# Forgetting attention: logit biases loaded from shifted copies in place of being added up on GpSimd

## The chip, the cores and the metric

The kernel runs on one core of one Trainium2 chip. A core has TensorE (PE, matrix products into PSUM), VectorE (DVE), ScalarE (ACT), GpSimd (POOL) and SyncE (SP), each with an instruction queue of its own that is worked through in order; semaphores tie the queues together. SyncE issues almost all transfers between HBM and the on-chip memory SBUF; 16 DMA engines carry them. The metric is device time in microseconds for one execution, the median over several runs; lower is better.

## The reference

A decoder trunk of two layers over 512 tokens of width 1024, in float32. Layer 0 mixes tokens with a gated unit (gMLP), layer 1 with Forgetting Attention (FoX, 16 heads of 64); each is followed by a squared-ReLU MLP of width 4096, and every part adds to the residual `x`. The change lies in the attention alone:

```python
q, k, v, gate, f_logit = jnp.split(h @ w_in, [W, 2 * W, 3 * W, 4 * W], axis=-1)
...
log_f = jax.nn.log_sigmoid((f_logit + b_f).astype(jnp.float32))
c = jnp.cumsum(log_f, axis=1).transpose(0, 2, 1)
...
for i in range(S // Q_BLOCK):
    q0 = i * Q_BLOCK
    kend = q0 + Q_BLOCK
...
    logits = jnp.einsum('bhtd,bhsd->bhts', qb, kb).astype(jnp.float32) * scale
    logits = logits + c[:, :, q0:kend, None] - c[:, :, None, :kend]
    logits = jnp.where(t_idx >= s_idx, logits, -jnp.inf)
    probs = jax.nn.softmax(logits, axis=-1).astype(vb.dtype)
```

`c` holds, for each head, the running sum over tokens of the log forget gates. A logit of query t and key s gets `c[t] - c[s]`. The term `c[t]` is the same over a whole row, and a softmax doesn't change when a constant is added to a row.

## The kernel before

Every weight is split into a high and a low part (`wh`, `wl`), and each product is made of three matmuls (`mm3`). Weights come in chunks through `Stream`: SyncE loads a chunk into one of three `raw` buffers (line 80), ScalarE rounds it into `wh` (line 85), and the rest `wl` is formed (line 86), in the attention stage by GpSimd, in the others by VectorE. The next load into a `raw` buffer waits for the `wl` that read it last. `wh` and `wl` have four buffers each, and the stream runs three chunks ahead of use.

The attention stage (`fs` and `fp` pools, lines 605 to 902) works on 8 pairs of heads, p = 0 to 7, and 4 blocks of 128 queries, i = 0 to 3. Block i sees keys 0 to (i+1)·128. `project` makes queries, keys and values of a pair; its tail takes the mean squares of queries and keys (`yss`), raises them to a power on GpSimd (line 725) and scales `y` on VectorE (line 726). `forget`, run once with pair 0, makes the log forget gates, sums them by two matmuls into `pc`, keeps the negative sums in `ct` (queries on partitions; line 645), transposes them into `pct`, copies them to `cs` (heads on partitions, line 651) and writes `cs` to HBM as `cd` (line 652).

`attend` then works on one pair. It transposes `y` (`tq`, `tk`), forms `qs`, `ks`, `kl`, and for each of its two heads, e = 0 and 1, with hd = 2p + e: loads `cd[hd]` broadcast over all 128 partitions into `cb` (line 785), and for each block GpSimd adds `ct` to a stretch of `cb` (line 792) and masks the diagonal (line 794) to get `bias`. TensorE makes the logits `lg` with the sign turned round, VectorE adds the bias and takes the row minimum (line 803, `ee` and `mn`), ScalarE takes the exponential with its row sum (line 804), and VectorE scales by the reciprocal of that sum (lines 806 and 808). The `bias` tiles have one buffer for each i, `cb` has two. The weights `ee` are transposed (`tp`, line 840), split into `pth` and `ptl` (lines 842, 843) and multiplied with the values (`ot`); the result is gated (line 828) and split (lines 859, 860).

Several of these generators run interleaved with the projections. `advance` steps the one that is due by the counter `order["us"]`, which only `placed` moves, that is only matmuls and transposes of this stage; those are kept in the order of the program. The other engines' orders are fixed when the program is built, by a planner that has its own estimate of when things are ready and prefers what comes first in the program. Tiles of one tag share that tag's buffers: a tile that takes a buffer waits until the last reader of the tile before is done.

Of the kernel before, what the change touches and what calls it, by code (L numbers as in the profile page):

```python
# [8 lines left out]
F32 = mybir.dt.float32  # L9
F32R = mybir.dt.float32r  # L10
AF = mybir.ActivationFunctionType
ALU = mybir.AluOpType
# [4 lines left out]
P = 128  # L17
D = 1024
S = 512
KB = D // P  # L20
NT = S // P
E = 2 * D
FF = 4 * D
H = 16
# [114 lines left out]
def trunk(ctx: ExitStack, tc: tile.TileContext, A, out, stages=4):  # L139
    nc = tc.nc  # L140
    pe, dve, act, pool = nc.tensor, nc.vector, nc.scalar, nc.gpsimd
# [6 lines left out]
    dram = ctx.enter_context(tc.tile_pool(name="dram", bufs=1, space=DRAM))  # L148
# [4 lines left out]
    def psB(name):  # L153
        return ps.tile([P, S], F32, tag="B", name=name, bufs=3)

    def psD(name):
        return ps.tile([P, S], F32, tag="D", name=name, bufs=1)
# [83 lines left out]
    def mm(dst, a, b, start, stop, more=False):  # L241

        ins = pe.matmul(dst, a, b, start=start, stop=stop, skip_group_check=more)  # L243
        placed(ins, dst.shape[-1])
        return ins

    def turn(dst, src):
        placed(pe.transpose(dst, src, ident[: src.shape[0], : src.shape[0]]), 256)  # L248
# [357 lines left out]
    with ExitStack() as st:  # L606
        fs = st.enter_context(tc.tile_pool(name="fs", bufs=2))
        fp = st.enter_context(tc.tile_pool(name="fp", bufs=2))
# [11 lines left out]
        for e in range(2):  # L620
            dve.memset(kl[e][(1 - e) * DH : (2 - e) * DH].bitcast(F32), 0.0)
        ct = fp.tile([P, NT, H], F32, tag="ct", name="ct", bufs=1)
        cd = dram.tile([H, S], F32, tag="cd", name="cd")

        def forget(pq):

            fl = fp.tile([P, NT, H], F32, tag="fl", name="fl", bufs=1)
            for i in range(NT):
                dve.scalar_tensor_tensor(fl[:, i], pq[i][:, 3 * P : 3 * P + H], nm.rstd[:, i : i + 1], bf, op0=ALU.mult, op1=ALU.add)
            ff = fl.rearrange("p i h -> p (i h)")  # L630
            fa = fp.tile([P, NT * H], F32, tag="fa", name="fa", bufs=1)
            dve.scalar_tensor_tensor(fa, ff, -1.0, ff, op0=ALU.mult, op1=ALU.min)
            act.activation(fa, fa, AF.Exp)
            act.activation(fa, fa, AF.Ln, bias=1.0)
            dve.scalar_tensor_tensor(ff, ff, 0.0, fa, op0=ALU.min, op1=ALU.subtract)

            pre = fp.tile([P, NT, H], F32, tag="pre", name="pre", bufs=1)
            dve.memset(pre[:, 0], 0.0)
            for i in range(1, NT):
                dve.tensor_tensor(pre[:, i], pre[:, i - 1], fl[:, i - 1], op=ALU.add)  # L640
            yield LAG_FORGET, None
            pc = psD("pc")
            mm(pc[:, : NT * H], tri, ff, True, False)
            mm(pc[:, : NT * H], ones, pre.rearrange("p i h -> p (i h)"), False, True)
            dve.tensor_scalar(ct.rearrange("p i h -> p (i h)"), pc[:, : NT * H], -1.0, None, op0=ALU.mult)
            yield LAG_PT, None
            pt = psD("pct")
            for i in range(NT):
                turn(pt[:H, i * P : (i + 1) * P], ct[:, i])
            cs = fp.tile([H, S], F32, tag="oz", name="cs")  # L650
            act.activation(cs, pt[:H], AF.Copy, scale=-1.0)
            nc.sync.dma_start(cd, cs)
            did.add("F")

        epsr = small.tile([P, NT], F32, tag="epsr", name="epsr")
# [35 lines left out]
        def project(p, values=True):  # L691
# [9 lines left out]
            if p == 0:  # L701
                dve.tensor_scalar(epsr, nm.ms, RMS_EPS, None, op0=ALU.mult)
                running.append([order["us"], forget(pq), None])
                advance(True)
                gates[0] = gate_act(0, gates[0])
                did.add(("G", 0))
# [18 lines left out]
            pool.tensor_tensor(sf, sf, mhalf, op=ALU.pow)  # L725
            dve.tensor_tensor(yh, yh, sf.unsqueeze(2).to_broadcast([P, NT * 4, DH]), op=ALU.mult)  # L726
            running.append([order["us"] + LAG_NORM, attend(p, y), None])

        def gate_act(p, pg):
# [28 lines left out]
        def attend(p, y):  # L758
# [21 lines left out]
            for e in range(2):  # L780
                hd = 2 * p + e
                yield lag, ("T", p - 1, e) if p else "F"
                lag = 0.0
                cb = fp.tile([P, S], F32, tag="cb", name=f"cb{hd}")
                nc.sync.dma_start(cb, cd[hd].partition_broadcast(P))
                ees = []
                sm = fs.tile([P, NT], F32, tag="sm", name=f"sm{hd}")
                mn = fs.tile([P, NT], F32, tag="mn", name=f"mn{hd}")
                for i in range(NT):
                    n = (i + 1) * P  # L790
                    bi = fp.tile([P, n], F32, tag=f"bias{i}", name=f"bias{hd}_{i}", bufs=1)
                    pool.tensor_scalar(bi, cb[:, :n], 1.0, ct[:, i, hd : hd + 1], op0=ALU.mult, op1=ALU.add)
                    dg = bi[:, i * P :]
                    pool.affine_select(dg, dg, pattern=[[-1, P]], compare_op=ALU.is_ge, fill=BIG, base=0, channel_multiplier=1)
                    yield lag, None
                    lag = LAG_LOGIT * rush
                    ee = fp.tile([P, n], F32, tag=f"ee{i}", name=f"ee{hd}_{i}", bufs=2)
                    ees.append(ee)
                    lg = psB(f"lg{hd}_{i}")
                    ts_ = slice(i * P, (i + 1) * P)  # L800
                    mm(lg[:, :n], qs[e][:, ts_], ks[e][:, :n], True, False)
                    mm(lg[:, :n], qs[e][:, ts_], kl[e][:, :n], False, True)
                    dve.tensor_tensor_reduce(ee, lg[:, :n], bi, 1.0, 3.0e38, op0=ALU.add, op1=ALU.min, accum_out=mn[:, i : i + 1])
                    act.activation(ee, ee, AF.Exp, bias=mn[:, i : i + 1], scale=-1.0, accum_out=sm[:, i : i + 1])
                rc = fs.tile([P, NT], F32, tag="rc", name=f"rc{hd}")
                dve.reciprocal(rc, sm)
                for i in range(NT):
                    dve.tensor_scalar(ees[i], ees[i], rc[:, i : i + 1], None, op0=ALU.mult)  # L808
                soft.append(ees)
                did.add(("L", p, e))  # L810
# [19 lines left out]
            for e in range(2):  # L830
                hd = 2 * p + e
# [4 lines left out]
                for j in range(NT):  # L836
                    n = (NT - j) * P
# [118 lines left out]
def build(arrays, stages=4):  # L956
    import concourse.bacc as _bacc

    nc = _bacc.Bacc("TRN2", target_bir_lowering=False, num_devices=1)
    args = {}  # L960
    for name, a in arrays.items():
        args[name] = nc.dram_tensor(f"in_{name}_dram", a.shape, mybir.dt.from_np(a.dtype), kind="ExternalInput").ap()
    out = nc.dram_tensor("out_0_dram", (D, S), F32, kind="ExternalOutput").ap()
    with tile.TileContext(nc, schedule_with_timeline_sim=True) as tc:
        trunk(tc, args, out, stages)
    return nc
# [9 lines left out]
```

## Time and profile before

| | us |
|---|---|
| median of 3 runs | 1277.18 |
| lowest, highest | 1276.97, 1279.51 |
| the profiled execution, time | 1277.01 |
| the profiled execution, span of its instructions | 1275.3 |

The page gives the span, the busy time of each engine, and groups of instructions by line of the kernel. "Idle before" is the time in which an engine had nothing to run before an instruction of the group, and the name behind the arrow is what ended that. The timeline view lists instructions as start, duration, engine, line, operation, output and inputs, shape and count, with the idle time before in brackets. The windows view gives, for a stretch, the busy time of PE, PEld (weight loads of TensorE), DVE, ACT and POOL, then the granted clock, the share of time in which the DMA engines were busy, and GB/s. In the views of waits the numbers behind the colon are microseconds in total, how many times, and the longest. Lines of DMA issues have the size of each and the median time from issue to landing. SPq is SyncE's queue.

### The profile page before, as it was taken

How to read it: one execution, taken by the hardware profiler on the slowest of the kernel's cores; microseconds unless marked ns; L12 is line 12 of the kernel's file. 1: busy time of each engine (PE TensorE's matmuls, PEld its weight loads, DVE VectorE, ACT ScalarE, POOL GpSimd, SP SyncE). 2: the span in 40 equal slices, each digit the busy share in tenths (PEclk: the TensorE clock that was granted, in tenths of full speed). 3: DMA queues.
4: the chain of work that ended last, by engine and by line, in shares of the span. 5: the costliest groups of instructions: out<-in, count | busy, mean ns of one | idle time of the engine just before them, and what ended most of it. 6: DMA issues, size and time to landing. Idle time of an engine off the chain costs nothing.

```text
span 1275.3 us, 18354 instructions
## 1 busy us (share of the span) xinstructions
PE 1262.1 (99%) x7108; PEld 1114.0 (87%) x7108; DVE 877.2 (69%) x1206; ACT 624.9 (49%) x981; POOL 484.7 (38%) x415
## 2 busy tenths in 40 slices
PE   9999999999999999999999999999999999999998
PEld 7888888888999999998899899898888999999987
DVE  7347767677867676765537777777887767676763
ACT  7334423246534344443467687678465444444430
POOL 4108433025423232310657667667173322323200
PEclk9999999999999999999999999999999999999999
DMA  7333233233233332323223222223223323232321
GB/s 250 97 107 92 83 91 91 84 98 93 90 116 100 100 102 97 111 89 96 80 81 103 84 82 76 84 77 106 83 67 116 116 84 116 84 116 83 118 81 66
DMA packets 39607, 124.01 MB, mean 97 GB/s; under 512 B 4816, under 2 KB 5840, under 8 KB 39520
## 3 DMA queue, kind: packets, MB, share of 16 engines
q1 hardware_dynamic: 39232, 122.82, 30.4%
q8 instruction: 56, 0.92, 0.3%
q14 instruction: 31, 0.25, 0.1%
q10 hardware_dynamic: 288, 0.02, 0.0%
HBM read 120.69 MB, written 2.13 MB: 96 GB/s over the span
## 4 chain that ended last, share of the span: by engine, by line
PE 89%; DVE 6%; ACT 2%; issue 1%; POOL 1%; DMA 1%; DVEq 0%; ACTq 0%; POOLq 0%
PE po L243 36%; PE da L243 11%; PE bc L243 9%; PE pq L243 8%; PE pv L243 8%; PE pu L243 7%; PE ph L243 3%; PE pg L243 2%; PE ot L243 2%; DVE xl L271 1%; PE lg L243 1%; PE tp L248 1%; PE sp L426 1%; DVE ee L808 1%; DVE y L726 1%
## 5 line engine op out<-in xcount | busy, mean ns | idle before, releaser
L85 ACT ACTIVATE wh<-raw 128x1024 fp32r<-128x1024 f32 (+3 forms) x230 | 219.7, 957 | 270.9 <-PE po L243 83.5
L86 DVE TENSOR_TENSOR wl<-raw,wh 128x1024 fp32r<-128x1024 f32 (+1 forms) x178 | 252.5, 1432 | 46.2 <-ACT wh L85 45.4
L243 PE MATMUL po<-zl,wh 128*128 128x512 f32 x512 | 200.6, 392 | 1.3 <-DVE zl L500 1.3
L243 PE MATMUL po<-zh,wh 128*128 128x512 f32 x512 | 199.9, 391 | 0.0
L243 PE MATMUL po<-zh,wl 128*128 128x512 f32 x512 | 199.5, 390 | 0.0
L556 DVE TENSOR_TENSOR x<-x,po 128x512 f32<-128x512 f32 x128 | 87.2, 683 | 106.1 <-PE po L243 106.1
L86 POOL TENSOR_TENSOR wl<-raw,wh 128x768 fp32r<-128x768 f32 (+3 forms) x52 | 102.4, 1969 | 125.7 <-ACT wh L85 123.2
L110 POOL TENSOR_TENSOR ssum<-raw 128x512 f32<-128x512 f32 x26 | 35.5, 1364 | 268.6 <-DMA raw<-in_m_dram 256.8
L85 ACT ACTIVATE sh<-ssum 128x1024 fp32r<-128x1024 f32 x52 | 55.2, 1061 | 164.5 <-POOL ssum L111 95.8
L243 PEld LDWEIGHTS po<-zh,wl 128*128 128x128 f32 x512 | 96.2, 188 | 19.5
L243 PEld LDWEIGHTS po<-zh,wh 128*128 128x128 f32 x512 | 96.5, 188 | 17.9
L243 PEld LDWEIGHTS po<-zl,wh 128*128 128x128 f32 x512 | 96.6, 189 | 17.8 <-DVE zl L500 1.6
L243 PE MATMUL pq<-wh,xh 128*128 128x384 f32 (+2 forms) x256 | 88.4, 345 | 0.0
L410 POOL TENSOR_SCALAR vn<-v,mv,lnr 128x128 f32<-128x128 f32 x64 | 63.1, 999 | 59.5 <-DVE vl L414 59.4
L243 PE MATMUL pq<-wh,xl 128*128 128x384 f32 (+2 forms) x256 | 83.1, 325 | 0.0
L243 PE MATMUL pq<-wl,xh 128*128 128x384 f32 (+2 forms) x256 | 82.7, 323 | 0.0
L86 DVE TENSOR_TENSOR sl<-ssum,sh 128x1024 fp32r<-128x1024 f32 x52 | 65.9, 1268 | 18.2 <-ACT sh L85 18.1
L112 POOL TENSOR_TENSOR ssum<-raw,ssum 128x512 f32<-128x512 f32 x26 | 37.1, 1428 | 69.1 <-DVE sl L86 68.8
L243 PE MATMUL da<-th,sl 128*128 128x256 f32 x208 | 58.9, 283 | 0.0
L243 PE MATMUL da<-tl,sh 128*128 128x256 f32 x208 | 58.8, 283 | 0.0
L243 PE MATMUL pv<-wh,xh 128*128 128x512 f32 (+1 forms) x160 | 58.0, 372 | 0.7 <-ACT wh L85 0.7
L243 PE MATMUL pv<-wl,xh 128*128 128x512 f32 (+1 forms) x160 | 58.7, 368 | 0.0
(212 smaller groups left out, 3489.9 us busy)
## 6 DMA issues: line engine op xcount, KB each, us to landing
raw<-in_m_dram SPq DMA_DIRECT2D x128, 512.0 KB, 3.6
raw<-in_gw_u_dram SPq DMA_DIRECT2D x16, 512.0 KB, 3.5
raw<-in_gw_o_dram SPq DMA_DIRECT2D x16, 512.0 KB, 3.5
raw<-in_fw_qkv_dram SPq DMA_DIRECT2D x20, 384.0 KB, 3.0
raw<-in_gw_v_dram SPq DMA_DIRECT2D x14, 512.0 KB, 3.9
raw<-in_fw_g_dram SPq DMA_DIRECT2D x8, 512.0 KB, 3.4
cb<-cd SPq DMA_DIRECT2D x16, 256.0 KB, 3.3
raw<-in_fw_o_dram SPq DMA_DIRECT2D x8, 512.0 KB, 3.5
```

The source lines that it names most:

```text
L85: self.nc.scalar.activation(hi, t, AF.Copy)
L86: eng.tensor_tensor(lo, t, hi.bitcast(F32), op=ALU.subtract)
L110: tt(s12[:, 0], a21, a22, op=ALU.add)
L112: tt(s43[:, 0], a12, s12[:, 1], op=ALU.subtract)
L243: ins = pe.matmul(dst, a, b, start=start, stop=stop, skip_group_check=more)
L248: placed(pe.transpose(dst, src, ident[: src.shape[0], : src.shape[0]]), 256)
L271: dve.scalar_tensor_tensor(l, x[b], gcol, h.bitcast(F32), op0=ALU.mult, op1=ALU.subtract)
L410: pool.tensor_scalar(vn[:, i], v[i][:, cb * P : (cb + 1) * P], mv[:, i, 0:1], lnr[:, i : i + 1], op0=ALU.subtract, op1=ALU.mult)
L426: pe.matmul(dst, vh[:, 2 * c + i], wide, start=True, stop=False)
L556: dve.tensor_tensor(x[b], x[b], pt, op=ALU.add)
L726: dve.tensor_tensor(yh, yh, sf.unsqueeze(2).to_broadcast([P, NT * 4, DH]), op=ALU.mult)
L808: dve.tensor_scalar(ees[i], ees[i], rc[:, i : i + 1], None, op0=ALU.mult)
```

## The change

`forget` no longer writes one copy of the running sums. VectorE makes four, one for each block of queries: the sums up to the end of the block, less the sum at the block's first token. Each is written to its own place in `cd`. For each head and block, one transfer then brings that copy's row, broadcast over the partitions, straight into the `bias` tile; GpSimd's addition of `ct` goes, and its masking of the diagonal stays. What differs from the bias before is a constant for each row, which the softmax takes out again. `cb` goes; `bias` tiles of the first three blocks have two buffers, that of the fourth has one. The shifted copies pass through the same buffers.

```diff
-        cd = dram.tile([H, S], F32, tag="cd", name="cd")
+        cd = dram.tile([H, NT, S], F32, tag="cd", name="cd")
+
+        def bias_tile(i, name):
+            return fp.tile([P, (i + 1) * P], F32, tag=f"bias{i}", name=name, bufs=2 if i < 3 else 1)
...
             act.activation(cs, pt[:H], AF.Copy, scale=-1.0)
-            nc.sync.dma_start(cd, cs)
+            for i in range(NT):
+                n = (i + 1) * P
+                shifted = bias_tile(i, f"cs{i}")
+                dve.tensor_scalar(shifted[:H], cs[:, :n], cs[:, i * P : i * P + 1], None, op0=ALU.subtract)
+                nc.sync.dma_start(cd[:, i, :n], shifted[:H])
             did.add("F")
...
-                cb = fp.tile([P, S], F32, tag="cb", name=f"cb{hd}")
-                nc.sync.dma_start(cb, cd[hd].partition_broadcast(P))
+                bias = []
+                for i in range(NT):
+                    bias.append(bias_tile(i, f"bias{hd}_{i}"))
+                    nc.sync.dma_start(bias[i], cd[hd, i, : (i + 1) * P].partition_broadcast(P))
...
                 for i in range(NT):
                     n = (i + 1) * P
-                    bi = fp.tile([P, n], F32, tag=f"bias{i}", name=f"bias{hd}_{i}", bufs=1)
-                    pool.tensor_scalar(bi, cb[:, :n], 1.0, ct[:, i, hd : hd + 1], op0=ALU.mult, op1=ALU.add)
+                    bi = bias[i]
                     dg = bi[:, i * P :]
```

## The prediction

> **What bounds the kernel now.** I read the busy times first, then what TensorE waits for in the attention stage, then what stands in front of those waits.
>
> ```profile
> span 1275.3 us, 18354 instructions
> PE 1262.1 (99%) x7108; PEld 1114.0 (87%) x7108; DVE 877.2 (69%) x1206; ACT 624.9 (49%) x981; POOL 484.7 (38%) x415
> ...
> 655.00:900.00 245.00, 239.36 (x1471) 219.63 (x1471) 180.92 (x417) 183.73 (x392) 162.94 (x178) 1.00 0.28 87
> ...
> PE tp L248 <- DVE ptl L843: 3.6, 4, 1.9
> PE tq L248 <- DVE y L726: 1.0, 2, 0.7
> PE ot L243 <- DVE v L677: 0.6, 1, 0.6
> ```
>
> The third line is the row of the windows view for 655 to 900 us, the stretch in which the biases are made: TensorE (PE) is busy 239.4 of 245 us, VectorE (DVE) 180.9, GpSimd (POOL, the last number with a count) 162.9, at full clock. The last three lines are, but for 0.2 us, all that TensorE waits for between 640 and 900 us: 5.2 us, every time for VectorE, never for GpSimd, a DMA or a weight. So TensorE bounds this stage too, and the change touches none of its work. The order of matmuls is set by a counter that only matmuls and transposes advance, and the change leaves every `yield` where it was, so I take TensorE's order as unchanged. What the change can give is part of those 5.2 us. What it can take is larger.
>
> **What is removed.**
>
> ```profile
> L792 POOL TENSOR_SCALAR bias<-cb,ct 128x128 f32<-128x128 f32 (+1 forms) x64 | 38.4, 606 | 18.1 <-DVE mn L803 12.3 <-DVE kl L775 4.6 <-DVE yss L724 1.2
> L794 POOL TENSOR_SCALAR_AFFINE_SELECT bias<-bias 128x128 f32<-128x128 f32 x64 | 22.0, 355 | 1.3
> ...
>   POOL bias L794: 1.5, 2
> ...
> POOL wl L86 <- ACT wh L85: 69.0, 22, 5.6
> ACT wh L85 <- PE po L243: 9.0, 4, 4.4
> ACT wh L85 <- PE pq L243: 8.7, 5, 4.2
> ```
>
> The 64 additions go: 38.4 us of GpSimd, whose load in the stretch falls from 162.9 to about 124.5. The 64 masks stay. Directly this is worth almost nothing: VectorE stood idle for a bias for 1.5 us, twice (third line, from the view of the tile `bias`). Nor is the weight path short of GpSimd: it waits 69 us for ScalarE's halves (`wh`), and ScalarE waits for TensorE to free their buffers (last two lines). Weights are ahead of use, so earlier `wl` gives nothing.
>
> The gain is indirect: VectorE runs slower while GpSimd is busy.
>
> ```profile
> 707.13 2.74 DVE L808 TENSOR_SCALAR ee<-ee,rc 128x128 f32<-128x128 f32 x4
> ...
> 712.16 1.27 DVE L808 TENSOR_SCALAR ee<-ee,rc 128x128 f32<-128x128 f32 x4
> ...
> 706.33 1.85 POOL L86 TENSOR_TENSOR wl<-raw,wh 128x768 fp32r<-128x768 f32 x1
> 708.15 1.07 POOL L792 TENSOR_SCALAR bias<-cb,ct 128x256 f32<-128x256 f32 x2
> 709.19 0.83 POOL L794 TENSOR_SCALAR_AFFINE_SELECT bias<-bias 128x128 f32<-128x128 f32 x2
> 711.83 2.91 POOL L725 TENSOR_TENSOR yss<-yss,mhalf 128x16 f32<-128x16 f32 x1
> ...
> 714.78 0.30 PE L248 MATMUL tp<-ident,ee 128*128 128x128 f32 x1 [1.87 <-DVE ptl L843]
> ```
>
> The same four scalings of one head took 2.74 us beside GpSimd's `wl`, additions and masks, and 1.27 us beside its power (L725). The excess is 1.47 us. Shared out by overlap (1.05 us of `wl`, 1.07 of additions, 0.68 of masks), the additions' part is 1.07/2.80 x 1.47 = 0.56 us. It lies in VectorE's queue ahead of the largest wait of TensorE, 1.87 us at 714.78, so I take it as **0.56 us saved**. The second place is the last pair:
>
> ```profile
> 884.49 2.04 DVE L808 TENSOR_SCALAR ee<-ee,rc 128x128 f32<-128x128 f32 x4
> ...
> 884.89 0.59 POOL L794 TENSOR_SCALAR_AFFINE_SELECT bias<-bias 128x128 f32<-128x128 f32 x2
> 885.47 0.78 POOL L792 TENSOR_SCALAR bias<-cb,ct 128x512 f32<-128x512 f32 x1
> 886.22 2.54 POOL L86 TENSOR_TENSOR wl<-raw,wh 128x1024 fp32r<-128x1024 f32 x1
> ...
> 887.19 0.50 PE L243 MATMUL ot<-pth,v 128*128 128x512 f32 x1 [0.62 <-DVE v L677]
> ```
>
> Here the excess is 2.04 - 1.27 = 0.77 us, and the addition covers 0.75 of the 2.04 us, so 0.75/2.04 x 0.77 = **0.28 us saved** ahead of a wait of 0.62. Elsewhere VectorE's saving ends in no wait of TensorE, or the slow neighbour is `wl`, which stays. The bounds of this term: nothing, if `wl` moves into the freed place and slows VectorE there instead; and the whole of the waits that lie behind attention work, 3.6 + 0.6 + 0.3 = 4.5 us (of the two waits for `y` the longer, 0.7, is the first pair's, and its `y` starts when L725 ends). I take 0.8 because that is what overlap shows.
>
> The page GPSIMD Engine Reference of the Trainium skill (section Specifications) limits this contention to VectorE instructions that use both ports or two SBUF inputs. By it the scalings and `y` gain but the additions of logits and bias (L803), with one input in PSUM, do not; if the rule were void and L803 gained too, the sum would only move towards the fast rival.
>
> **What is added at the start.** Four VectorE subtractions on 16 partitions, 128 to 512 columns, and four writes in place of one.
>
> ```profile
> 659.59 0.57 ACT L651 ACTIVATE cs<-pct 16x512 f32<-16x512 f32 x1
> ...
> 660.00 2.85 DVE L726 TENSOR_TENSOR y<-y,yss 128x1024 f32<-128x1024 f32 x1 [1.72 <-POOL yss L725]
> 664.32 0.74 DVE L774 SCALAR_TENSOR_TENSOR qs<-tq,qkn,qs 64x512 fp32r<-64x512 f32 x1 [1.47 <-ACT qs L771]
> ...
> cd<-cs SPq DMA_DIRECT2D x1, 32.0 KB, 2.0
> cb<-cd SPq DMA_DIRECT2D x16, 256.0 KB, 3.3
> ```
>
> The nearest row is again the scaling of four blocks: 1.27 us as the value, 2.74 as the upper end, nothing as the lower. `cs` is finished at 660.16, when VectorE has begun `y` at 660.00; behind `y` it idles 1.47 us up to 664.32. I put the subtractions there, 662.85 to 664.12: **0 us**. If the order of VectorE were made the other way round, `y` would start at 660.16 + 1.27 = 661.43, and TensorE, which waits for `y`, would lose 1.4 us.
>
> The writes then land by about 664.1 + 2.0 = 666.1, and the first block's bias (64 KB, between the rows for 32 and 256 KB, so 2.0 to 3.3) by 668.1 to 669.4; with the mask of 0.36 us it is ready by 669.8 at the latest. The last block's bias, three SyncE (SP) issues of about 0.4 us later, is ready by 671.0.
>
> ```profile
> 669.23 0.29 DVE L803 CUSTOM_DVE_ANT_0 ee<-lg,bias 128x128 f32<-128x128 f32 x1
> ...
> 671.23 0.56 DVE L803 CUSTOM_DVE_ANT_0 ee<-lg,bias 128x384 f32<-128x384 f32 x1 [0.96 <-POOL bias L794]
> 672.74 0.69 DVE L803 CUSTOM_DVE_ANT_0 ee<-lg,bias 128x512 f32<-128x512 f32 x1 [0.94 <-PE lg L243]
> ```
>
> So the first head may start 0.6 us late, and VectorE's own idle 0.96 and 0.94 us in the third and fourth block take that up: 0 us. Without that cover it would be 0.6.
>
> **What is added per head.** Each head now loads 64 + 128 + 192 + 256 = 640 KB in place of 256: 16 x 384 KB = 6.3 MB more, 26 GB/s beside 87, so DMA engines busy 0.28 go to about 0.36. The 48 more issues hold SyncE 16 us in all (0.33 each); behind them in its queue stand weight loads, which have the cover shown above. These are **0 us**.
>
> The new wait that matters is that of the fourth block. Its bias has a single buffer, so for the second head of a pair the load is issued only when VectorE has used the first head's. Queued behind it on SyncE are weight loads; queued behind its mask on GpSimd are `wl` and the power. Who waits for it is VectorE's queue. The price: landing 3.3 us (the first line below, of the view of the tile `cb`, has 3.0 to 4.3) plus mask 0.36, so 3.66 us, or 4.66 at the worst landing. The distances are those between two 512-column rows of L803:
>
> ```profile
> DMA to landing us min/median/max: 3.0/3.3/4.3
> ...
> 679.62 0.68 DVE L803 CUSTOM_DVE_ANT_0 ee<-lg,bias 128x512 f32<-128x512 f32 x1
> ...
> 704.04 0.68 DVE L803 CUSTOM_DVE_ANT_0 ee<-lg,bias 128x512 f32<-128x512 f32 x1
> ...
> 710.38 0.68 DVE L803 CUSTOM_DVE_ANT_0 ee<-lg,bias 128x512 f32<-128x512 f32 x1
> ...
> 857.34 0.69 DVE L803 CUSTOM_DVE_ANT_0 ee<-lg,bias 128x512 f32<-128x512 f32 x1
> ...
> 862.30 0.68 DVE L803 CUSTOM_DVE_ANT_0 ee<-lg,bias 128x512 f32<-128x512 f32 x1
> ```
>
> In pair 0 there are 679.62 - 673.43 = 6.2 us (the first head's stands above, at 672.74), in pair 1 710.38 - 704.72 = 5.7, in pair 6, the shortest that I found, 862.30 - 858.03 = 4.3. The slack is 2.5, 2.0 and 0.6 us (1.0 less at the worst landing, so at most 0.4 lost in pair 6): **0 us**, as long as SyncE is free when the buffer is. [...] The three smaller biases have two buffers and are free a pair earlier.
>
> **Sum.** 0.56 + 0.28 = 0.84 saved, nothing lost. The profiled execution took 1277.01 us (1.7 beside its span), the median of the three is 1277.18; 1277.0 - 0.8 = **1276.2 us**. A measurement can tell about 0.2% (2.55 us) from no change, so this counts as none.
>
> **The rivals.**
> *Slower: the fourth block's load is stuck behind a weight load.* SyncE takes its queue in order, and a weight load at its head waits for `wl`.
>
> ```profile
> 708.20 0.33 SPq L80 DMA_DIRECT2D raw<-in_fw_qkv_dram  x1
> ...
> 863.09 3.48 SPq L80 DMA_DIRECT2D raw<-in_fw_o_dram  x2
> ```
>
> If pair 1's load stands behind the one at 708.20, it is issued at 708.53 and ready at 712.2: 1.8 us after 710.38. Pair 6's behind 863.09 is issued at 863.42 and ready at 867.1: 4.8 us late. Together 6.6 us, counted in full since VectorE is behind TensorE there: 1276.2 + 6.6 = 1282.8. It decides from an issue 2.0 us (pair 1) or 0.6 us (pair 6) after the buffer comes free. For it: the slack is thin, the order is fixed when the program is built. Against: `wl` comes earlier on a lighter GpSimd, so these loads do too.
> *Faster: nearly all waits behind VectorE go*, since `wl` also moves out of the scalings' way: 4.5 us less, 1272.5. For it: scalings took 1.27 to 2.74 us. Against: `wl` is the larger part of the overlap and stays.
> *Unchanged to slightly slower*: `wl` slides into the freed place, or the subtractions go ahead of `y`: 1277.0 to 1278.4.
>
> **Chances.** Forecast 0.42, unchanged 0.08, faster rival 0.22, slower rival 0.28. The forecast and the unchanged case lie within 0.2%. So faster 0.22, same 0.50, slower 0.28. The range takes in both rivals with a microsecond for their sizes: 1271.5 to 1284.0; the likeliest case's own is 1274.8 to 1278.4.
>
> **What would show it.** Right: GpSimd down by about 38 us, L808 shorter in the mean, TensorE's wait at `tp` in pair 1 shorter than 1.87 us, no bias named among VectorE's waits, `y` starting at 660. Wrong: VectorE waiting for a mask at a 512-column L803, or a bias load issued right behind a weight load and microseconds after its buffer was free (slow rival); TensorE's waits for VectorE near 1 us (fast rival); TensorE's instructions in another order, which would void the whole sum.

## The result and the profile after

The changed kernel took **1285.59 us** (median of 5 runs, 1284.54 to 1289.51) against 1277.18 before (5 runs, 1276.26 to 1279.51): a ratio of 1.0068, with a 95% interval of 1.0049 to 1.0087. It is slower by 8.4 us, where 1276.2 was forecast. The profiled execution took 1284.54 us with a span of 1282.8, so its trace holds 7.5 us of the 8.4. Its granted clock is 1.000; the other four runs have 0.997 to 0.999.

First the page of the kernel after: the span, and the busy time of each engine.

```profile
span 1282.8 us, 18419 instructions
...
PE 1263.2 (98%) x7108; PEld 1114.7 (87%) x7108; DVE 879.3 (69%) x1210; ACT 624.6 (49%) x981; POOL 448.2 (35%) x351
```

GpSimd does 36.5 us less (484.7 before), as forecast. No engine does noticeably more, and the number of TensorE's matmuls and their order are the same. So the 7.5 us are waits. The windows view of the stretch from 655 to 900 us, and the view of what TensorE waited for between 600 and 960 us (total, times, longest):

```profile
655.00:900.00 245.00, 231.37 (x1430) 213.24 (x1429) 175.18 (x407) 180.39 (x386) 121.09 (x113) 1.00 0.36 111
```

```profile
PE tp L248 <- DVE ptl L852: 8.6, 7, 2.0
PE ot L243 <- DVE v L685: 2.7, 1, 2.7
PE tq L248 <- DVE y L734: 1.1, 2, 0.7
PE tq L248 <- DVE ptl L852: 0.6, 1, 0.6
...
PE ot L243 <- DVE oz L836: 0.5, 1, 0.5
PE po L243 <- DVE v L685: 0.4, 1, 0.4
```

TensorE is busy 231.4 us of the 245 where it was 239.4. The waits are 13.9 us where they were 5.2: 8.7 more, all for VectorE. (The span grows by 7.5 only; a wait for `zl` later in the kernel falls from 1.3 to 0.2 us.) Set side by side matmul by matmul, the two traces show where TensorE falls behind: by 1.9 us in pair 0, by 1.0 to 1.2 in each of pairs 1, 2 and 3, by 2.9 in the last pair, and by little elsewhere. VectorE is hardly busier (879.3 us, 877.2 before), so it must be late: it waits itself. For whom, the view of all waits from 640 to 930 us of the kernel after says:

```profile
POOL bias L803 <- DMA bias<-cd: 39.0, 24, 6.5
...
DVE y L734 <- POOL yss L733: 9.4, 6, 2.6
...
DVE ee L812 <- POOL bias L803: 4.6, 4, 1.8
```

and the same view of the kernel before:

```profile
DVE y L726 <- POOL yss L725: 3.7, 4, 1.7
...
DVE ee L803 <- POOL bias L794: 1.5, 2, 1.0
```

GpSimd, which has less to do, stands still for 39 us with a mask (line 803) at the head of its queue, waiting for its bias to land. VectorE in turn waits 9.4 us for GpSimd's power and 4.6 us for masks, 5.2 before. Here is one such place, the end of pair 0, in the timeline of the kernel after (start, duration, in brackets the idle time before and what ended it; first SyncE, then GpSimd, then VectorE):

```profile
675.44 0.33 SPq L80 DMA_DIRECT2D raw<-in_fw_g_dram  x1
675.87 0.38 SPq L795 DMA_DIRECT2D bias<-cd  x1
```

```profile
678.71 0.29 POOL L803 TENSOR_SCALAR_AFFINE_SELECT bias<-bias 128x128 f32<-128x128 f32 x1 [2.03 <-DMA bias<-cd]
678.97 1.84 POOL L86 TENSOR_TENSOR wl<-raw,wh 128x768 fp32r<-128x768 f32 x1
...
685.89 0.29 POOL L803 TENSOR_SCALAR_AFFINE_SELECT bias<-bias 128x128 f32<-128x128 f32 x1 [0.47 <-DMA bias<-cd]
686.15 1.83 POOL L86 TENSOR_TENSOR wl<-raw,wh 128x768 fp32r<-128x768 f32 x1
687.95 2.90 POOL L733 TENSOR_TENSOR yss<-yss,mhalf 128x16 f32<-128x16 f32 x1
```

```profile
681.09 0.69 DVE L812 CUSTOM_DVE_ANT_0 ee<-lg,bias 128x512 f32<-128x512 f32 x1 [1.82 <-POOL bias L803]
...
690.88 3.40 DVE L734 TENSOR_TENSOR y<-y,yss 128x1024 f32<-128x1024 f32 x1 [2.56 <-POOL yss L733]
```

In the order of GpSimd's queue the mask at 678.71 belongs to pair 1, whose logit for it comes 26 us later (704.88); its load was issued early because its buffer was free. GpSimd waits 2.03 us for it. Behind it stand `wl`, and behind that the mask of pair 0's fourth block, which VectorE needs now: VectorE idles 1.82 us. The queue is only part of this wait. The fourth block's own load was issued at 675.87, 2.1 us after its single buffer came free (673.76), right behind a weight load on SyncE (675.44), and took 4.6 us to land, until 680.5: with nothing ahead of it on GpSimd its mask would have been some 0.3 us earlier. Then more masks of pair 1, the last one at 685.89 waiting for its landing, and another `wl` stand ahead of pair 1's power, whose input was ready at 685.7 (line 732 ends there) and which starts at 687.95. `y` is late by as much, and VectorE's queue has `y` ahead of the `ptl` that TensorE needs next. TensorE loses 1.55 us at 685.66 (0.42 before) and 0.62 at 694.80 (none before).

In pair 1 a mask of pair 2 holds `wl` back by 2.83 us:

```profile
709.56 0.43 POOL L803 TENSOR_SCALAR_AFFINE_SELECT bias<-bias 128x128 f32<-128x128 f32 x1 [2.83 <-DMA bias<-cd]
```

That `wl` falls upon pair 1's scalings: 2.90 us for four that take 1.27 beside the power (714.50 in this same trace: 1.28). That is little more than the 2.74 us of before, and TensorE's wait behind them, 1.97 us at 717.12, was 1.87. What the change adds in pair 1 comes next, by the same second mechanism on another instruction:

```profile
717.24 1.84 POOL L86 TENSOR_TENSOR wl<-raw,wh 128x768 fp32r<-128x768 f32 x1
```

```profile
717.35 2.81 DVE L734 TENSOR_TENSOR y<-y,yss 128x1024 f32<-128x1024 f32 x1
```

```profile
720.55 0.55 PE L248 MATMUL tp<-ident,ee 128*128 128x128 f32 x3 [1.66 <-DVE ptl L852]
```

A mask that waited 0.50 us for its landing stands ahead of `wl`, which so starts just before `y`. `y` takes 2.81 us beside it (1.22 in e1 below, without a `wl` beside it), and now stands ahead of a `ptl` that came before it in the kernel before; TensorE waits 1.66 us for that `ptl`, where it waited 0.71 for the next one.

The last pair shows the second mechanism alone: no mask waits, but GpSimd, free of additions, starts `wl` at once.

```profile
891.18 2.56 POOL L86 TENSOR_TENSOR wl<-raw,wh 128x1024 fp32r<-128x1024 f32 x1 [0.33 <-ACT wh L85]
```

```profile
890.39 3.63 DVE L817 TENSOR_SCALAR ee<-ee,rc 128x128 f32<-128x128 f32 x4
```

```profile
895.16 0.50 PE L243 MATMUL ot<-pth,v 128*128 128x512 f32 x1 [2.69 <-DVE v L685]
```

Before, masks and the 512-column addition (884.89 to 886.22) stood ahead of that `wl`, and the four scalings took 2.04 us; TensorE waited 0.62 at the same place.

### The profile page after: what moved, and what is told of

Same layout as the page of the kernel before. It is cut to its first block, busy times and chain, and to the rows that moved or that the text cites. A ratio compares the mean times of both kernels' runs of the same rounds, so it can differ in the third digit from the quotient of the medians.

```text
span 1282.8 us, 18419 instructions
## 1 busy us (share of the span) xinstructions
PE 1263.2 (98%) x7108; PEld 1114.7 (87%) x7108; DVE 879.3 (69%) x1210; ACT 624.6 (49%) x981; POOL 448.2 (35%) x351
## 4 chain that ended last, share of the span: by engine, by line
PE 85%; DVE 7%; POOL 2%; DMA 2%; ACT 2%; issue 1%; SPq 0%; POOLq 0%; DVEq 0%; ACTq 0%
PE po L243 36%; PE da L243 11%; PE bc L243 9%; PE pv L243 7%; PE pu L243 7%; PE pq L243 7%; PE ph L243 3%; DMA bias<-cd 2%; PE ot L243 1%; PE pg L243 1%; DVE xl L271 1%; DVE y L734 1%; POOL yss L733 1%; DVE ee L817 1%; PE lg L243 1%
```

## The experiments

Four explanations were put against each other. **A**: masks wait for landings in GpSimd's queue, and hold up what stands behind them. **B**: the single buffer of the fourth block makes its load late. **C**: the added transfers, or SyncE's 48 more issues, cost the time. **D**: `wl` falls on VectorE's scalings and stops them. In the diffs, "after" is the changed kernel. Each was timed against the kernel before in the same session (1277.05 to 1277.25 there).

**e1: the masks of a pair behind that pair's power** (A). TensorE's and ScalarE's orders stay as they are; on VectorE two neighbours change places, on SyncE one weight load.

```diff
-            pool.tensor_tensor(sf, sf, mhalf, op=ALU.pow)
+            powers[p] = pool.tensor_tensor(sf, sf, mhalf, op=ALU.pow).ins
...
-                    pool.affine_select(dg, dg, ...)
+                    with tc.issue_after(powers[p]):
+                        pool.affine_select(dg, dg, ...)
```

> The changed kernel, but on GpSimd the masks of a pair stand behind that pair's power (L733), so that a mask for the next pair, whose bias is still in flight, can no longer stand in front of the power or of weight rests that are wanted now. Theory A (GpSimd's queue is held up by masks that wait for a landing): about 1277, at most 1279, GpSimd's idle time for landings of bias falls from 39 us to under 15, and the power of the second pair starts within 0.3 us of its input instead of 2.3 us after. Theory B (the single buffer of the fourth block is what is late): nothing changes, 1284 to 1287, since the fourth block's wait in a pair stays. Theory C (the additional transfers and SyncE's longer queue): 1284 to 1287.

Measured: 1278.08 us (11 runs, 1277.02 to 1281.66), ratio 1.0011 (1.0002 to 1.0020): 7.5 of the 8.4 us are gone, with the same masks, the same transfers and the same buffers. TensorE's waits, and GpSimd's masks from 655 to 908 us (busy, mean ns, then the idle time before them and its causes), in this kernel:

```profile
PE tp L248 <- DVE ptl L853: 3.7, 5, 1.8
PE ot L243 <- DVE v L685: 2.7, 1, 2.7
```

```profile
L804 POOL TENSOR_SCALAR_AFFINE_SELECT bias<-bias 128x128 f32<-128x128 f32 x64 | 24.3, 410 | 24.7 <-DMA bias<-cd 24.6
```

The waits at `tp` are back at 3.7 us (8.6 after, 3.6 before), though the trace is that of the longest of the eleven runs (1281.66). GpSimd still waits 24.6 us for landings (under 15 was expected), but the power no longer stands behind them: VectorE waits 3.4 us for it, 9.4 before the edit. In pair 0 a wait of 1.82 us at `tp` stays: the fourth block's mask itself waits 3.40 us for its landing there (682.49). The wait at `ot` is untouched: 2.7.

**e2, e4: no masks at all**, in the kernel after (e2) and, as a control, in the kernel before (e4).

```diff
-                    pool.affine_select(dg, dg, ...)
```

> The changed kernel without the 64 masks of the diagonal (left out, so the weights above the diagonal are not zero). GpSimd then waits for no landing at all; VectorE waits for the loads itself. Theory A: 1274 to 1278. Theory B: the fourth block's load is still issued late; 1282 to 1286. Theory C: 1283 to 1286. To be read against the kernel before without its masks.

> The kernel before without its 64 masks (left out, as in the run above). It is the yardstick for that run: 22 us of GpSimd go in both. All theories: 1274 to 1277.5. Theory A has the two within 2 us of each other; theory C has the changed kernel without masks some 8 us longer; theory B 5 to 8.

Measured: the kernel after without masks 1279.65 us (11 runs), ratio 1.0019 (1.0010 to 1.0028), 1.7 us above the range of A; its wait at `ot` is still 2.7. The kernel before without masks **1287.54** (5 runs), ratio 1.0078 (1.0065 to 1.0090): 22 us of GpSimd's work left out, no wait for a landing anywhere, and 10 us slower. That was a surprise, and it speaks for D. The control's waits of TensorE, and its last pair:

```profile
PE tp L248 <- DVE ptl L842: 8.8, 7, 2.5
PE ot L243 <- DVE v L677: 3.2, 1, 3.2
```

```profile
889.74 2.40 POOL L86 TENSOR_TENSOR wl<-raw,wh 128x1024 fp32r<-128x1024 f32 x1
```

```profile
888.64 3.71 DVE L807 TENSOR_SCALAR ee<-ee,rc 128x128 f32<-128x128 f32 x3
```

Three scalings begun at 888.64 end at 892.35, just after `wl` (892.14). The two kernels also speak against C: without masks the kernel after, with all its transfers and issues, is 8 us faster than the kernel before. e13 below settles it: it has them all and is faster than the kernel before with its masks.

**e3: two buffers for the fourth block** (B); the second block gives one up for room.

```diff
-            return fp.tile([P, (i + 1) * P], F32, tag=f"bias{i}", name=name, bufs=2 if i < 3 else 1)
+            return fp.tile([P, (i + 1) * P], F32, tag=f"bias{i}", name=name, bufs=1 if i == 1 else 2)
```

> The changed kernel with two buffers for the biases of blocks 1, 3 and 4 and one for the second block (the memory does not hold two for all). Theory A: 1283 to 1287, even more masks can stand ahead. Theory B: the loss of the fourth block goes; 1280 or less, no wait of VectorE for a mask at a 512-column row. Theory C: 1284 to 1287.

Measured: 1287.44 us (5 runs, 1283.77 to 1289.27), ratio 1.0074 (1.0061 to 1.0088): not faster. GpSimd waits even longer for landings, 45.1 us. B falls as the explanation of the 8.4 us. In pair 0 it does hold: the logits of the fourth block no longer wait for a mask there (679.53), and TensorE's wait at `tp` is 0.78 us in place of 1.55. Next to it, at `tq`, 0.62 became 2.24. The trace's waits add up to 14.1 us, 13.9 in the kernel after; with them goes a granted clock of 0.91 in the stretches 680 to 700 and 740 to 760 us, where the trace of the kernel after has 1.00. The run moves the single buffer to another block rather than taking it away, so it says nothing on a kernel with two buffers everywhere.

**e8: the addition kept as idle work**: does more GpSimd work keep `wl` off the scalings, as the additions did before?

```diff
+                    pool.tensor_scalar(bi, bi, 1.0, None, op0=ALU.mult)
                     pool.affine_select(dg, dg, ...)
```

> The changed kernel with GpSimd's 38 us put back: each bias, loaded finished, is multiplied by 1 in place before its mask (64 instructions of the same shapes). Theory D in its plain form (GpSimd's removed work had kept the rests away from VectorE's scalings): back towards 1277 to 1281. Theory A: the additional instructions wait for the same landings and hold the queue longer, 1286 to 1292. Theory C: 1285 to 1288.

Measured: 1305.3 us (5 runs), ratio 1.0223 (1.0209 to 1.0237). That lies above every range given for it (A had 1286 to 1292). More work on GpSimd as such protects nothing: here it waits for landings too (26.5 us), in the same queue, and makes everything behind it later still. This fits A; why it costs so much more than A foresaw stays open.

**m1: the standstill by itself** (D): a small kernel in place of the decoder, twelve VectorE instructions of each kind, first alone (`q_`), then while GpSimd works through 24 subtractions of 1024 columns (`b_`).

> No decoder at all: it leaves out the whole computation and hands x through. Four kinds of VectorE instruction, twelve of each, first with GpSimd idle and then beside a row of GpSimd subtractions of 128x1024. Theory D: the scaling with one SBUF input (128x512) takes about 0.48 us alone and 2 to 3 us beside GpSimd; the sum of two SBUF inputs 0.6 to 0.7 alone and more beside; the sum with one input in PSUM the same both times. If the slowing were a plain sharing of bandwidth, all with SBUF inputs would slow by one factor under 2 instead.

Measured, in its groups by line (busy us, mean ns of one):

```profile
L52 POOL TENSOR_TENSOR w<-w,w 128x1024 f32<-128x1024 f32 x24 | 60.9, 2536 | 1.9
L42 DVE TENSOR_TENSOR b_two_in<-x,x 128x512 f32<-128x512 f32 x12 | 32.6, 2720 | 0.4
L40 DVE TENSOR_SCALAR b_one_in<-x,one 128x512 f32<-128x512 f32 x12 | 27.4, 2281 | 0.4
L42 DVE TENSOR_TENSOR q_two_in<-x,x 128x512 f32<-128x512 f32 x12 | 8.3, 691 | 0.4
L44 DVE TENSOR_TENSOR q_psum<-bank,x 128x512 f32<-128x512 f32 x12 | 8.3, 690 | 0.4
L44 DVE TENSOR_TENSOR b_psum<-bank,x 128x512 f32<-128x512 f32 x12 | 8.3, 690 | 0.4
L40 DVE TENSOR_SCALAR q_one_in<-x,one 128x512 f32<-128x512 f32 x12 | 5.8, 486 | 0.4
```

A scaling of 512 columns takes 486 ns alone and 2281 beside GpSimd; a `tensor_tensor` with both inputs in SBUF 691 and 2720. The 24 VectorE instructions together lasted 60.0 us, the 24 of GpSimd 60.9: VectorE gets one instruction done for each of GpSimd's. So this isn't a slowdown by a share but a standstill until GpSimd's instruction ends. An input in PSUM is spared (690 both times, though only the first three of the twelve ran beside GpSimd, which had finished by then).

**e5, e6: `wl` in halves**: if a standstill lasts until GpSimd's instruction ends, shorter ones should let VectorE through.

```diff
+                for q in (slice(0, h), slice(h, n)):
+                    eng.tensor_tensor(lo[:, q], t[:, q], hi[:, q].bitcast(F32), op=ALU.subtract)
```

> The changed kernel, with each weight rest (wl) of the attention stage made by two GpSimd instructions of half the columns instead of one. Theory D (a VectorE instruction that needs both SBUF ports stands still until the GpSimd instruction under way ends, and the change has moved the rests of 1.8 to 2.5 us onto scalings, squares and y that stand ahead of TensorE's transposes): the longest such standstill is halved, about 1280 to 1282, and the last pair's wait of TensorE at ot falls from 2.7 us to 1.4 to 1.7. Theory A alone (masks wait for a landing in GpSimd's queue): no better than the changed kernel, 1285 to 1288, as GpSimd has more to do. Theory C (transfers): 1285 to 1287.

> Halved rests and, on GpSimd, the masks of a pair behind that pair's power: both remedies at once. If A and D are both at work: below both remedies alone, 1274 to 1277, TensorE's wait at ot in the last pair 1.7 us or less. If only A: as with the masks' place alone, 1278 to 1279. If only D: as with the halves alone.

Measured: on the kernel after 1285.99 us (5 runs), ratio 1.0069 (1.0056 to 1.0081); with the masks behind the power as well 1279.2 (11 runs), ratio 1.0017 (1.0008 to 1.0025). Nothing gained. The last pair's four scalings take 3.71 us (3.63 whole) and the wait at `ot` is 2.8 us, where 1.4 to 1.7 was expected: VectorE gets one instruction in between the halves and then stands again.

**e9 to e12: scalings on ScalarE**: the first head's of the last pair, on e1 (e9) and on the kernel after (e12); of the first and the last pair (e10) and of all pairs (e11), both on e1.

```diff
-                    dve.tensor_scalar(ees[i], ees[i], rc[:, i : i + 1], None, op0=ALU.mult)
+                    if (p, e) == (7, 0):
+                        act.activation(ees[i], ees[i], AF.Copy, scale=rc[:, i : i + 1])
+                    else:
+                        dve.tensor_scalar(ees[i], ees[i], rc[:, i : i + 1], None, op0=ALU.mult)
```

> Masks behind the power, and the four scalings of the last pair's first head on ScalarE instead of VectorE, where a weight rest of 2.6 us on GpSimd held one of them up. Theory A with D: TensorE's wait at ot in the last pair falls from 2.7 us to under 0.7, the time by 2 to 2.5 us against the masks' place alone: 1275 to 1276.5, not slower than the kernel before. Theory A alone (the standstill isn't what TensorE waits for): 1277.5 to 1279, the wait at ot stays.

> The changed kernel as it is, with only the last pair's first head scaled on ScalarE: D's part in the loss by itself. D: 1283 to 1284, 2 to 2.5 us less than the changed kernel, wait at ot under 0.7. Theory A alone: 1285 to 1286.

> As above, and the first pair's first head scaled on ScalarE too (one of its scalings stood 1.95 us under a weight rest with the masks moved; TensorE then waited 1.8 us at tp). A with D: 1 to 1.5 us less than with the last pair alone, 1274 to 1275.5. A alone: the same as with the last pair alone.

> Masks behind the power and the first head's scalings of all eight pairs on ScalarE: 32 scalings, about 14 us of ScalarE more and as much of VectorE less. D: 1273.5 to 1275.5, TensorE's waits for VectorE in the stage under 5 us. If ScalarE's queue becomes late with it (its exponentials stand behind the scalings): 1276 to 1280.

Measured: 1279.86 us (11 runs), ratio 1.0019 (1.0010 to 1.0027); on the kernel after 1287.77 (6 runs), 1.0090 (1.0075 to 1.0105); two pairs 1279.45 (11 runs), 1.0018 (1.0009 to 1.0027); all pairs 1285.2 (5 runs), 1.0054 (1.0042 to 1.0066). No gain in any. TensorE's waits with the last pair's on ScalarE, on e1:

```profile
PE ot L243 <- DVE v L685: 1.7, 1, 1.7
PE po L243 <- DVE v L685: 1.3, 1, 1.3
```

The lateness has moved, not gone: ScalarE also makes the high half of `v`, which now stands behind the scalings (2.69 + 0.38 us became 1.66 + 1.28). Behind these two waits the granted clock falls: 0.83 from 880 to 900 us, where e1's trace has 1.00. Side by side, TensorE loses 2.0 us more there than in e1. So these runs don't test D; the remedy is dearer than what it cures.

**e13: the last pair's `wl` behind a mask** (D, a cleaner test): on e1, the subtraction that starts 0.2 us ahead of the 512-column scaling is queued behind the mask of the second head's fourth block; the four masks of that head are issued together. The edge is in GpSimd's queue alone; VectorE's order shifts in the last pair, where the second head's scalings go ahead of two halves of `v`.

```diff
-        eng.tensor_tensor(lo, t, hi.bitcast(F32), op=ALU.subtract)
+        if self.behind is None or eng is not self.nc.gpsimd:
+            eng.tensor_tensor(lo, t, hi.bitcast(F32), op=ALU.subtract)
+            return
+        with self.tc.issue_after(self.behind):
+            eng.tensor_tensor(lo, t, hi.bitcast(F32), op=ALU.subtract)
+        self.behind = None
...
+                    elif i == 0:
+                        for j in range(NT):
+                            dj = bias[j][:, j * P :]
+                            with tc.issue_after(powers[p]):
+                                masked = pool.affine_select(dj, dj, ...)
+                        ws.behind = masked.ins
```

> e1 with one GpSimd instruction moved: in the last pair, the weight subtraction (wl, 128x1024) that e1 starts at 887.22 us, 0.2 us ahead of the 512-column scaling of the pair's first head, is queued behind the mask of the second head's fourth block (whose load was issued at 884.17 and lands about 3.4 us later, so that the mask ends near 888.0). TensorE's order is that of e1; on VectorE the second head's last logit and scalings go ahead of the last two halves of v7. Theory D (a scaling stands still until the GpSimd tensor_tensor that runs beside it ends): the four scalings take 1.3 us in place of 3.63, the last of them 0.47, TensorE's wait at ot falls from 2.7 us to about 0.6, and the time from 1278.1 to some 1276.0, level with or under the kernel before. Theory A alone (only masks that wait for landings in GpSimd's queue cost time): nothing is left to gain there, 1278.1 within 0.8, the wait at ot as in e1. If the scalings are short but the time is not, the wait has moved to v7 or to the weights behind the held subtraction.

Measured: **1275.39 us** (11 runs, 1274.48 to 1276.21), ratio 0.9987 (0.9978 to 0.9996). That is 2.7 us under e1 and 1.7 under the kernel before, faster than both kernels, though by less than 0.2%. Its last pair, then TensorE's waits:

```profile
883.28 0.31 POOL L817 TENSOR_SCALAR_AFFINE_SELECT bias<-bias 128x128 f32<-128x128 f32 x1 [0.51 <-DMA bias<-cd]
883.56 2.56 POOL L91 TENSOR_TENSOR wl<-raw,wh 128x1024 fp32r<-128x1024 f32 x1
```

```profile
882.31 1.56 DVE L832 TENSOR_SCALAR ee<-ee,rc 128x128 f32<-128x128 f32 x4
```

```profile
PE tp L255 <- DVE ptl L867: 3.2, 5, 1.2
...
PE ot L250 <- DVE v L692: 0.6, 1, 0.6
```

The mask, which waits for its landing until 883.28, now holds `wl` off the scalings: 1.56 us for the four in place of 3.63, and the wait at `ot` is 0.6 in place of 2.7. D is shown for this place. The weights behind that `wl` were not missed. Of the 2.7 us, the waits of the last pair show 1.9 (at `ot` and `po` 3.6 us in e1, 1.7 here). The rest isn't placed; all 11 runs of e13 have a granted clock of 1.000, those of e1 0.998 to 1.000.

**e14: the same edge alone**, on the kernel after (the masks' order left as the change has it).

> The changed kernel with the one instruction of e13_hold_wl moved and nothing else: the last pair's weight subtraction stands behind the mask of the second head's fourth block; all other masks stay where the change has them. If the two mechanisms add up, this gains what e13 gained over e1, 2.7 us, and keeps what e1 took away, 7.5 us: 1285.6 - 2.7 = 1282.9, the wait at ot 0.6 in place of 2.7, the waits at tp and tq as in the changed kernel (8.6 and 1.1). If the moved instruction helped only because e1 had reordered the masks, 1285.6.

Measured: 1283.71 us (6 runs, 1281.75 to 1289.79), ratio 1.0063 (1.0047 to 1.0080); waits of 0.6 at `ot` and 7.8 at `tp` (after: 2.7 and 8.6). The gain is 1.9 us by the medians, 2.7 expected. The six runs spread over 8 us: the two longest, 1287.38 and 1289.79, have granted clocks of 0.997 and 0.996, the other four 0.999 and 1.000 and at most 1283.80. The waits of the last pair fall by 1.9 us here too (3.6 to 1.7). So the two costs add up, as well as can be measured:

| last pair's `wl` | masks as in the change | masks behind the power |
|---|---|---|
| as in the change | 1285.6 | 1278.1 |
| behind a mask | 1283.7 | 1275.4 |

## Why the prediction was wrong

By the table, the change's 8.4 us are +7.5 from the place of masks that wait in GpSimd's queue (A, with whatever standstills their place brought about), +1.9 to +2.7 from `wl` on the last pair's scalings (D), and a rest of -1.0 to -1.8 us. The prediction's sum has neither of the two costs.

- **TensorE bounds the stage, and its order stays**: right.
- **The gain of 0.56 + 0.28 us**: in pair 1 it is there once both costs are gone. In e13 the wait of 1.87 us at `tp` is 0.62, and the second one, 0.71 at 718.13, has gone: 2.0 us. But other waits grow as much (pair 0's from 0.42 to 1.23), and the view of TensorE's waits gives 5.6 us in all for e13, 5.2 for the kernel before. Pair 0's wait has a cause of its own: the fourth block's load again stands behind a weight load on SyncE, issued 2.0 us after its buffer came free (675.16, 673.20). The two spans differ by 1.3 us. Side by side matmul by matmul, e13 is 0.2 us ahead before the attention stage and 1.1 at the end: it gains 1.9 us in pair 1 and 1.8 in small steps in pairs 2 and 4 to 7, and loses 0.8 in pair 0, 0.7 in pair 3 and 1.3 behind the last pair's first `ot`. Whether the small gains belong to the change or to e13's edges stays open.
- **Pair 7's part of that gain** had the wrong sign. The prediction shared out the excess by overlap, as though each neighbour slowed the scalings in proportion. It is a standstill until the neighbour ends: what counted was that the addition kept `wl` from starting, and without it the wait at `ot` went from 0.62 to 2.69. The page SBUF — State Buffer of the Trainium skill (section Who interferes with whom) has this as a rule for VectorE in a two-port mode: whoever issues first gets the pair of ports that it shares with GpSimd for the whole instruction, and the other "fully blocks". The rows of the small kernel agree (2281 ns beside instructions of 2536); in which mode they ran no trace tells. The prediction named the contention and took only its reach, not its form. "`wl` slides into the freed place" stood among the rivals, with 0.08 and at most 1278.4.
- **The subtractions cost 0**: right. `y` started at 660.34 and they ran behind it:

```profile
660.34 2.85 DVE L734 TENSOR_TENSOR y<-y,yss 128x1024 f32<-128x1024 f32 x1 [1.72 <-POOL yss L733]
663.11 1.26 DVE L659 TENSOR_SCALAR cs<-cs 16x128 f32<-16x128 f32 x4
```

  The first head's logits came 0.3 to 1.3 us later (669.56 for the first block, 669.23 before; 672.50 for the third, 671.23 before), and TensorE didn't wait for them: right too.
- **6.3 MB more and 48 more issues cost 0**: right in themselves (landings of the biases 2.8 to 4.9 us, median 3.2, where 3.3 was taken; and e13, which has them all).
- **The step that failed**: "Queued behind it on SyncE are weight loads; queued behind its mask on GpSimd are `wl` and the power. Who waits for it is VectorE's queue." The prediction named what stands behind the mask, and then priced only the bias's own reader. It took the three smaller biases as harmless, since their buffers "are free a pair earlier". That is what did the harm: a load that can be issued a pair early makes a mask that enters GpSimd's queue a pair early and waits there for its landing, ahead of `wl`, of the power and of masks that are needed now. Before, the addition ahead of the mask took that place, and the row of line 792 names no DMA among what it waited for. Followed on to `wl`, the power and `y`, the added wait would have stood in the sum at up to a landing, 3.3 us, in each pair in which TensorE waits for VectorE, in place of 0; the two look-ahead masks shown above waited 2.03 and 2.83, and the masks' place cost 7.5 us in all.
- **The slower rival**, 1282.8, had the sign and nearly the size, but by another mechanism (a bias load stuck behind a weight load on SyncE, in pairs 1 and 6). In those two pairs the trace shows no such wait: the loads were issued at once (706.92 and 864.09, each 0.04 us after the buffer came free), and pair 6's distance was enough. In pair 0, which the prediction gave 2.5 us of slack, the mechanism did come true: an issue 2.1 us late behind a weight load and a landing of 4.6 us in place of 3.3. By e3 that is about 0.8 us at TensorE (1.55 and 0.78), not 6.6; so the rival's nearness to the measured time is luck.

What stays open: how far D accounts for waits at `tp` in pairs 0 to 6, where masks that wait decide when `wl` runs. A and D can't be told apart there; e1 took away both by its one edge. How much of the differences between runs of one kernel is the clock stays open as well, since only one run of each has a trace. And two buffers for every block, which might have made the change faster than e13, was not tried for want of room.

## What to carry to other kernels

When work of an engine that runs in order is replaced by a transfer, what is left on that engine (here a 0.3 us mask) changes from an instruction that is ready into one that waits: look at what stands behind it in the queue, at those issued early because a buffer was free above all, and pin them behind what is urgent. Less work on an engine off the critical path can cost time, when that work kept a long GpSimd instruction from starting under a short VectorE one. Where VectorE's inputs all lie in SBUF, as in the scalings and in `y`, count the time until GpSimd's instruction ends, not a share of it.

## What else the runs showed of the hardware

After a wait TensorE can run slowly for a few microseconds. In the kernel before without masks, the windows view from 860 to 908 us gives a granted clock (third number from the end) of 0.96:

```profile
860.00:908.00 48.00, 42.99 (x277) 38.20 (x276) 37.31 (x85) 32.53 (x73) 24.95 (x19) 0.96 0.28 89
```

and in its timeline two neighbouring matmuls of one kind, behind a wait of 3.17 us and again 4 us later:

```profile
893.88 0.50 PE L243 MATMUL ot<-pth,v 128*128 128x512 f32 x1 [3.17 <-DVE v L677]
...
897.36 0.63 PE L243 MATMUL po<-ol,wh 128*128 128x512 f32 x1
897.79 0.63 PE L243 MATMUL po<-oh,wl 128*128 128x512 f32 x1
...
901.24 0.40 PE L243 MATMUL po<-ol,wh 128*128 128x512 f32 x1
901.47 0.39 PE L243 MATMUL po<-oh,wl 128*128 128x512 f32 x1
```

They stand 0.43 us apart, then 0.23; from 897 to 899 us the granted clock is 0.50. A wait can so cost more than itself, and no view of waits shows the rest. The length of the wait alone doesn't decide it. In e1's trace the clock is 0.50 from 689 to 692 us, behind a wait of 1.82 us that ended at 687.40; in the trace of the kernel after it stays at 1.00 behind one of 2.69. The page TensorE: Matmul & The Clock Gate of the Trainium skill (section What's actually happening) states half the clock after an idle window of about 3.4 us; here waits of 3.17 and of 1.82 us sufficed.
